# A hybrid pooling/SSD decoder step on one core: earlier operand loads, one operand's low halves on another engine, and paired weight chunks in the second FFN product

## The chip, the core and the metric

The kernel runs on one core of one Trainium2 chip. A core has a matrix engine (TensorE, PE in the profile, with its weight loads shown as PEld), a vector engine (VectorE, DVE), a scalar engine (ScalarE, ACT), a general engine (GpSimd, POOL) and a queue engine (SyncE, SP) from which this kernel issues nearly all its transfers. The metric is device microseconds for one execution, the median of several runs.

## The reference: what is computed

One layer of a decoder trunk for a prompt of 1024 tokens and 64 sample tokens (8 sequences of 8), width 1024: a half-step SwiGLU FFN, a token mixer of two branches (causal pooling and a Mamba-2 SSD scan) merged by gates, a second half-step SwiGLU FFN, and a final RMSNorm.

```
def swiglu(x, w_in, w_out):
    gu = x @ w_in
    g, u = gu[..., :D_FF], gu[..., D_FF:]
    return (jax.nn.silu(g) * u) @ w_out          # D_FF = 2816, D_MODEL = 1024

x = x + 0.5 * swiglu(rmsnorm(x, norm_ffn1), ffn1_w_in, ffn1_w_out)
x = x + token_mixing(rmsnorm(x, norm_mix), ...)
x = x + 0.5 * swiglu(rmsnorm(x, norm_ffn2), ffn2_w_in, ffn2_w_out)
```

All arrays are float32. The change lies in the product with `w_out` alone, which runs twice, once in each FFN.

## The kernel before, in words

Every matrix product is done in three passes of a reduced-precision float32 type (F32R): an operand is split into a high half, a rounded copy made by ScalarE, and a low half, the difference, made as a rule by VectorE. The passes are high times high, weights' high times operand's low, and weights' low times operand's high.

The product with `w_out` is done "by sevens" (Strassen's scheme): both operands are cut in two by two blocks, and seven products of sums of blocks replace eight. `second` (from L767) runs the seven in the order `ORDER2 = "4251736"`; below they are called the first to the seventh product. The sums on the operand's side were formed earlier and lie in DRAM as `xq[p][kk]`, 11 tiles of 128x544 for each product (272 KB each). The sums on the weights' side are formed as they are needed. A product has two passes (`m0` = 0 and 2, each for 256 output columns), and a pass goes through 22 halves of the inner size in six **chunks**: five of two K-tiles and one of a single K-tile. For a chunk `second_weights` (L747 to L765) loads one or two raw blocks by SP (tile `wraw`, 256 KB a block, 6 buffers); where there are two, POOL adds or subtracts them into `ws` (L759, tag `wsum`, 4 buffers); ACT makes the high half `wh` (L763) and DVE the low half `wl` (L764), 3 buffers each. The first product ("4") and the sixth ("3") use a single raw block and have no sum on POOL; the other five use two.

With a chunk's weights there, PE (L177) runs, for each of two output tiles `j` and each K-tile, six matmuls of 272 columns: twelve for one `j` of a two-tile chunk, 24 a chunk, 264 a product. The results of a pass lie in four PSUM banks (two `j`, two column halves `c`); after a pass `add` (L810) scales them and adds them to the FFN's output tiles, mostly on DVE (L825, "evictions" below). In the sixth and seventh product all four banks come from a ring of six, so that the second `j` of a pass reuses the two banks of the first `j` of the pass before.

The operand of the next product is fetched while one runs (`fetch_x`, L772). Each step issues one load on SP (L786); the split into `hh`/`hp` (high, ACT, L776) and low half in place (L777) is emitted `X_LAG` = 4 steps later. The first step is due `X_AT` = 4.0 us (of modelled PE time) into the running product, and the steps are `X_PACE` = 1.8 us apart; for the last operand the delay is 15.0 and the pace 1.4. Operand tiles lie in a ring of 42 buffers (`act`), or, for products "4", "5" and "7", mostly in 8 pair buffers; a load waits until the earlier content has been read by PE. For the seventh product alone (`LO_POOL = "6"`) the low halves are made by POOL.

What is emitted in this order is then arranged by the framework's scheduler, which sets a fixed order for each engine's queue from its own estimates. At run time every engine takes its queue strictly in that order: an instruction that waits holds all behind it. On SP that means that an operand load that waits for its buffer holds the weight loads behind it, and on ACT that a split that waits for its load holds the next `wh`.

## Time and profile before

| what | value |
|---|---|
| median of 3 runs | 2902.27 us (2901.49 to 2903.34) |
| the profiled execution | 2906.4 us |
| its span, first to last instruction | 2904.6 us |
| PE busy in the span | 2788.6 us (96%) |
| second product of the first FFN | 528.7 to 787.7 us, 1848 matmuls |
| second product of the second FFN | 2624.1 to 2889.0 us, 1848 matmuls |

The profile shows one execution. Busy time of PE is that of pipelined matmuls, so the idle time in front of a matmul says more than the busy share: the view of waits gives, for each engine, how long it sat idle before an instruction and which other engine's instruction ended that wait. Since each stage has other limits, the views are read stage by stage, by windows in microseconds from the start of the span. In the first FFN the seven products begin at 528.7, 565.2, 599.4, 636.5, 672.1, 709.1 and 744.4 us; in the second at 2624.1, 2661.7, 2697.4, 2733.8, 2768.9, 2811.4 and 2850.9 us.

### The profile page before, as it was taken

To read this page: it belongs to the slowest core of one execution; us is meant where nothing else is said; L and a number is where in the kernel's file an instruction comes from. 1 tells how busy PE (TensorE), PEld (TensorE's weight loads), DVE (VectorE), ACT (ScalarE), POOL (GpSimd) and SP (SyncE) were. 2 spreads that over 40 slices of the span, in tenths; PEclk is the share of its full clock that TensorE was granted. 3 is DMA by queue.
4 is the path that set the end of the run, shared out by engine and by line. 5 is a ranking of instruction groups with operands and counts; after the bars stand their busy time and mean duration, and the time that the engine had idled before them with its cause. 6 is when DMAs were issued, how large, how long until landed. Compare 5 with 4: busy or idle time off the path is not lost. (4 is left out here: it accounts for less than half of the span.)

```text
span 2904.6 us, 54721 instructions
## 1 busy us (share of the span) xinstructions
PE 2788.6 (96%) x19834; PEld 2607.3 (90%) x19834; DVE 1878.8 (65%) x2890; ACT 1413.8 (49%) x3150; POOL 1400.8 (48%) x1428
## 2 busy tenths in 40 slices
PE   7999999999999999999999999899999999999997
PEld 6999999899889999999988887578999999999997
DVE  6556555776874586876766777766665454556754
ACT  5444444543454565554556566576233434445433
POOL 6566667442642355564622343332135666673424
PEclk9999999999999999999999999999999999999999
DMA  4565554787745455543376677785765332337855
GB/s 136 181 206 193 170 169 146 253 284 230 242 128 159 155 173 160 187 155 125 106 250 203 202 230 234 254 265 175 250 233 162 102 105 90 97 120 260 295 168 177
DMA packets 515791, 539.49 MB, mean 186 GB/s; under 512 B 41780, under 2 KB 356008, under 8 KB 515512
## 3 DMA queue, kind: packets, MB, share of 16 engines
q1 hardware_dynamic: 515504, 535.99, 57.6%
q8 instruction: 156, 2.56, 0.4%
q14 instruction: 115, 0.94, 0.1%
q10 hardware_dynamic: 16, 0.00, 0.0%
HBM read 383.43 MB, written 152.65 MB: 185 GB/s over the span
## 5 line engine op out<-in xcount | busy, mean ns | idle before, releaser
L177 PE MATMUL pw<-X,wh 128*128 128x288 f32 (+2 forms) x2832 | 627.4, 310 | 5.0 <-ACT v L576 2.6
L177 PEld LDWEIGHTS pw<-X,wh 128*128 128x128 f32 x2832 | 462.5, 190 | 26.9 <-ACT v L576 3.3
L177 PE MATMUL pw<-X,wl 128*128 128x288 f32 (+1 forms) x1644 | 473.8, 288 | 0.7 <-DVE wl L459 0.7
L459 DVE TENSOR_TENSOR wl<-s,wh 128x512 fp32r<-128x512 f32 x288 | 242.9, 845 | 248.3 <-ACT wh L458 237.0
L177 PE MATMUL pw<-hl,wh 128*128 128x256 f32 (+1 forms) x1536 | 391.6, 328 | 3.5 <-ACT t L580 2.3
L452 POOL TENSOR_TENSOR s<-wraw,wraw 128x512 f32<-128x512 f32 x144 | 198.1, 1376 | 331.6 <-DVE wl L459 215.0
L177 PE MATMUL pw<-hi,wh 128*128 128x288 f32 x1120 | 331.7, 296 | 2.7 <-DVE t L616 2.0
L177 PE MATMUL pw<-hi,wl 128*128 128x288 f32 x1120 | 329.8, 294 | 0.0
L177 PE MATMUL pw<-lo,wh 128*128 128x288 f32 x1120 | 329.7, 294 | 0.0
L177 PEld LDWEIGHTS pw<-X,wl 128*128 128x128 f32 x1644 | 311.8, 190 | 0.9 <-DVE wl L459 0.9
L177 PE MATMUL pw<-hl,wl 128*128 128x256 f32 x1072 | 300.6, 280 | 1.2 <-DVE wl L459 1.2
L177 PEld LDWEIGHTS pw<-hl,wh 128*128 128x128 f32 x1536 | 258.8, 189 | 24.7 <-ACT t L580 2.9
L759 POOL TENSOR_TENSOR ws<-wraw,wraw 128x512 f32<-128x512 f32 x120 | 166.9, 1399 | 225.1 <-DMA wraw<-in_ffn_w_out_dram 126.5
L459 DVE TENSOR_TENSOR wl<-wraw,wh 128x512 fp32r<-128x512 f32 x216 | 178.6, 827 | 123.3 <-ACT wh L458 121.0
L458 ACT ACTIVATE wh<-s 128x512 fp32r<-128x512 f32 x288 | 181.0, 629 | 137.9 <-PE pw L177 111.7
L177 PEld LDWEIGHTS pw<-hi,wh 128*128 128x128 f32 x1120 | 210.5, 188 | 9.6 <-DVE t L616 2.6
L177 PEld LDWEIGHTS pw<-lo,wh 128*128 128x128 f32 x1120 | 210.6, 188 | 0.0
L458 ACT ACTIVATE wh<-wraw 128x512 fp32r<-128x512 f32 x216 | 135.6, 628 | 154.0 <-PE pw L177 133.6
L177 PEld LDWEIGHTS pw<-hi,wl 128*128 128x128 f32 x1120 | 210.1, 188 | 0.0
L177 PEld LDWEIGHTS pw<-hl,wl 128*128 128x128 f32 x1072 | 203.0, 189 | 2.1 <-DVE wl L459 2.1
L177 PE MATMUL po<-hh,wh 128*128 128x272 f32 x848 | 180.2, 293 | 10.6 <-ACT wh L763 6.5
L177 PE MATMUL po<-hh,wl 128*128 128x272 f32 x848 | 178.9, 292 | 8.3 <-DVE wl L764 7.7
(403 smaller groups left out, 6872.9 us busy)
## 6 DMA issues: line engine op xcount, KB each, us to landing
wraw<-in_ffn_w_out_dram SPq DMA_DIRECT2D x240, 256.0 KB
wraw<-in_ffn_w_in_dram SPq DMA_DIRECT2D x188, 256.0 KB
wraw<-in_w_in_dram SPq DMA_DIRECT2D x144, 256.0 KB
wh<-part SPq DMA_DIRECT2D x116, 256.0 KB
wl<-part SPq DMA_DIRECT2D x116, 256.0 KB
hr<-xq SPq DMA_DIRECT2D x106, 272.0 KB
xq<-s SPq DMA_DIRECT2D x66, 272.0 KB
xq<-g SPq DMA_DIRECT2D x62, 272.0 KB
```

Source lines behind the costliest of these rows:

```text
L177: T.matmul(out, lhsT, rhs, start=start, stop=stop, skip_group_check=free)
L452: G.tensor_tensor(t, a, b, op=op)
L458: S.activation(wh, a, AF.Copy)
L459: V.tensor_tensor(wl, a, wh.bitcast(F32), op=ALU.subtract)
L759: G.tensor_tensor(s, raws[0], raws[1], op=ALU.subtract if p in MINUS2 else ALU.add)
```

## The change

Four things change in the second product, in both FFNs.

1. Operand loads: the first step comes 2.0 us into a product instead of 4.0, steps are 1.6 apart instead of 1.8, and the split is emitted six steps after the load instead of four. The last operand keeps a lag of four, its delay and its pace.
2. The low halves of the seventh product's operand are made by DVE instead of POOL: 11 instructions in each FFN.
3. The weights of single-block products (the first and the sixth) take their `wh` and `wl` from the `wsum` ring for two chunks in five, and from the rings of three for the other three.
4. In the sixth and seventh product the first two and the last two chunks of a pass are run as a pair: both chunks' weights are made, and then PE does all K-tiles of both for the first `j` and then for the second. A pass starts with 24 matmuls and ends with 18 on one `j`, instead of 12 and 6.

```diff
-LO_POOL = "6"
-X_AT, X_PACE, X_LAG = 4.0, 1.8, 4
+X_AT, X_PACE, X_LAG, X_LAG_END = 2.0, 1.6, 6, 4
...
             else:
                 s = raws[0]
-            wh, wl = (sp.tile([P, 4 * P], F32R, tag=t, bufs=N_W, name=nm(t))[:, : n2 * 2 * P] for t in ("wh", "wl"))
+            nth[0] += len(raws) == 1
+            if len(raws) > 1 or nth[0] % 5 < 3:
+                wh, wl = (sp.tile([P, 4 * P], F32R, tag=t, bufs=N_W, name=nm(t))[:, : n2 * 2 * P] for t in ("wh", "wl"))
+            else:
+                wh, wl = (stage["p"].tile([P, 4 * P], F32R, tag="wsum", bufs=N_S, name=nm(t))[:, : n2 * 2 * P] for t in ("wh", "wl"))
...
-                (G if p in LO_POOL else V).tensor_tensor(t[:, :n].bitcast(F32R), t[:, :n], a[:, :n].bitcast(F32), op=ALU.subtract)
+                V.tensor_tensor(t[:, :n].bitcast(F32R), t[:, :n], a[:, :n].bitcast(F32), op=ALU.subtract)
...
-                ahead.append(start(fetch_x(ORDER2[at + 1], range(NKK), 1.4 if last else X_PACE), 15.0 if last else X_AT if at else 6.0))
+                ahead.append(start(fetch_x(ORDER2[at + 1], range(NKK), *((1.4, X_LAG_END) if last else (X_PACE, X_LAG))),
+                                   15.0 if last else X_AT if at else 6.0))
...
-                for kp in range(0, NKK, 2):
-                    n2 = min(2, NKK - kp)
-                    W2 = second_weights(wo, p, kp, n2, m0)
+                kps = [(kp,) for kp in range(0, NKK, 2)]
+                if at >= 5:
+                    kps = [kps[0] + kps[1]] + kps[2:-2] + [kps[-2] + kps[-1]]
+                for run in kps:
+                    W2 = [(kp, min(2, NKK - kp), second_weights(wo, p, kp, min(2, NKK - kp), m0)) for kp in run]
                     for j in range(2):
-                        for k in range(n2):
+                        for kp, n2, W in W2:
+                            for k in range(n2):
...
```

The rest of the loop's body is the same with other indices. The change moves instructions on the queues; three places follow. Line numbers shift: L759, L763, L764, L776, L786 and L825 of the kernel before are L758, L766, L767, L779, L789 and L828 of the changed one.

The first place is ACT in the second FFN about the start of the fifth product (2764 to 2778 us). `hh_34198`, `hh_34231` and `hh_34265` are the splits of K-tiles 8, 9 and 10 of the sixth product's operand; `wh_33925` is the fifth product's second chunk and `wh_33964` its third. Before:

```order
L763 ACTIVATE wh_33887<-ws_33885 128x512
...
L776 ACTIVATE hh_34173<-hr_34172 128x544
L776 ACTIVATE hh_34198<-hr_34197 128x544
L763 ACTIVATE wh_33925<-ws_33923 128x512
L776 ACTIVATE hh_34231<-hr_34230 128x544
L763 ACTIVATE wh_33964<-ws_33962 128x512
L776 ACTIVATE hh_34265<-hr_34264 128x544
L763 ACTIVATE wh_34006<-ws_34004 128x512
```

Their loads on SP, before (`wraw_34116` and `wraw_34118` are the seventh chunk's blocks):

```order
L753 DMA wraw_34116<-in_ffn_w_out_dram 128x2x256
L753 DMA wraw_34118<-in_ffn_w_out_dram 128x2x256
L786 DMA hr_34197<-xq_8_337 128x544
L786 DMA hr_34230<-xq_9_338 128x544
L786 DMA hr_34264<-xq_10_339 128x544
```

The same two places after the change, ACT first (`wh_33926` and `wh_33967` are the second and third chunk) and then SP (`wraw_34003` to `wraw_34043` are the fourth and fifth chunk's blocks, `wraw_34080` and `wraw_34082` the sixth's, `wraw_34117` and `wraw_34119` the seventh's):

```order
L766 ACTIVATE wh_33885<-ws_33883 128x512
...
L779 ACTIVATE hh_34174<-hr_34173 128x544
L766 ACTIVATE wh_33926<-ws_33924 128x512
L779 ACTIVATE hh_34197<-hr_34196 128x544
L766 ACTIVATE wh_33967<-ws_33965 128x512
L766 ACTIVATE wh_34009<-ws_34007 128x512
```

```order
L789 DMA hr_34173<-xq_8_337 128x544
L752 DMA wraw_34003<-in_ffn_w_out_dram 128x2x256
...
L752 DMA wraw_34082<-in_ffn_w_out_dram 128x256
L789 DMA hr_34196<-xq_9_338 128x544
L803 DMA xr_34201<-xspill_3_94 128x576
L752 DMA wraw_34117<-in_ffn_w_out_dram 128x2x256
L752 DMA wraw_34119<-in_ffn_w_out_dram 128x2x256
L789 DMA hr_34231<-xq_10_339 128x544
```

K-tile 8 is now loaded four chunks earlier on SP and K-tile 9 one chunk earlier, K-tile 10 stays behind the seventh chunk's blocks, and its split has left the front of the fourth chunk's `wh`.

The second place is DVE in the first FFN from the sixth to the seventh product (about 744 us). `wl_9295` and `wl_9345` are the seventh product's first two weight chunks, the `x<-po` rows the evictions of the sixth product's second pass, `xn` and `hl` the norm in front of the mixer. Before:

```order
L764 TENSOR_TENSOR wl_9295<-ws_9292,wh_9294 128x512
L372 TENSOR_TENSOR hl_9323<-xn_9322,hl_9323 128x512
L965 SCALAR_TENSOR_TENSOR xn_9378<-x_6689,cols,r_9104 128x512
L764 TENSOR_TENSOR wl_9345<-ws_9342,wh_9344 128x512
L825 SCALAR_TENSOR_TENSOR x_6916<-po_9032,x_6916 128x272
L825 SCALAR_TENSOR_TENSOR x_6919<-po_9032,x_6919 128x272
```

After, where `hr<-hr,hh` are low halves that came from POOL and `wl_9305` is the second chunk:

```order
L780 TENSOR_TENSOR hr_9158<-hr_9158,hh_9159 128x544
L371 TENSOR_TENSOR hl_9260<-xn_9259,hl_9260 128x512
L828 SCALAR_TENSOR_TENSOR x_6912<-po_9032,x_6912 128x272
...
L828 SCALAR_TENSOR_TENSOR x_6925<-po_9035,x_6925 128x272
L767 TENSOR_TENSOR wl_9295<-ws_9292,wh_9294 128x512
L767 TENSOR_TENSOR wl_9305<-ws_9302,wh_9304 128x512
```

The eight evictions stood behind two `wl` and two norm steps, and now stand in front of the first `wl`.

The third place is POOL at the same point; in brackets stands whose progress the first sum of the seventh product waits for. Before, and then after:

```order
L759 TENSOR_TENSOR ws_9292<-wraw_9288,wraw_9290 128x512 [waits DMAHW7_49,DMAHW6_49,DVE_49]
```

```order
L758 TENSOR_TENSOR ws_9292<-wraw_9288,wraw_9290 128x512 [waits DMAHW6_49,DVE_49,DMAHW7_49,PE_49,Pool_49]
```

Since the sixth product's last two chunks now lie in the `wsum` ring, the first sums of the seventh take buffers that PE reads until nearly the end of the sixth; before, none of them waited for PE.

## The prediction

> **What bounds the kernel now.** I read the page's busy times, then the windows of the two second products, then PE's waits in each product, and last the timelines of the engine that each wait names.

> ```profile
> PE 2788.6 (96%) x19834; PEld 2607.3 (90%) x19834; DVE 1878.8 (65%) x2890; ACT 1413.8 (49%) x3150; POOL 1400.8 (48%) x1428
> ```
> ```profile
> core 0: us, PE busy (x) PEld busy (x) DVE busy (x) ACT busy (x) POOL busy (x), PEclk, DMA share, GB/s
> 528.00:565.00 37.00, 35.39 (x271) 34.26 (x269) 23.26 (x29) 17.43 (x39) 14.78 (x13) 1.00 0.80 262
> 565.00:599.00 34.00, 33.77 (x263) 33.18 (x262) 21.34 (x32) 17.70 (x41) 17.38 (x13) 1.00 0.94 311
> 744.00:788.00 44.00, 37.80 (x271) 36.23 (x269) 40.70 (x44) 19.51 (x36) 37.23 (x29) 0.92 0.80 252
> ```
> ```profile
> 2768.00:2811.00 43.00, 37.34 (x271) 36.80 (x270) 21.02 (x37) 9.20 (x16) 12.35 (x10) 0.88 0.47 151
> 2848.00:2889.00 41.00, 37.42 (x294) 36.56 (x293) 20.19 (x32) 13.07 (x27) 23.92 (x18) 1.00 0.42 128
> ```

> PE bounds the whole, so only its idle time can be saved. A product of 264 matmuls takes 34 us where it runs best (the first FFN's second product, at 94% DMA share), and 43 to 44 where it stalls. PE's waits in the products that the change aims at follow, in this order: first FFN, first, fifth and seventh product (windows 528 to 565, 672 to 709, 744 to 790).

> ```profile
> PE po L177 <- DVE wl L764: 0.9, 1, 0.9
> PE po L177 <- ACT wh L763: 0.7, 1, 0.7
> ...
> PE po L177 <- ACT wh L763: 1.5, 1, 1.5
> PE po L177 <- DVE wl L764: 1.0, 1, 1.0
> ...
> PE po L177 <- DVE x L825: 3.5, 1, 3.5
> PE po L177 <- DVE wl L764: 2.6, 2, 2.1
> ```

> Second FFN, first, fifth and seventh product (2624 to 2662, 2768 to 2811, 2848 to 2890):

> ```profile
> PE po L177 <- ACT wh L763: 2.4, 3, 1.6
> ...
> PE po L177 <- ACT wh L763: 4.1, 1, 4.1
> PE po L177 <- DVE wl L764: 1.6, 1, 1.6
> ...
> PE po L177 <- ACT wh L763: 2.0, 1, 2.0
> PE po L177 <- POOL hr L777: 1.4, 2, 0.7
> ```

> That is 1.6 and 2.4 us in the first products, 2.5 and 5.7 in the fifth, 6.1 and 3.4 in the seventh: 21.7 us in all, three quarters of a per cent of the span. In the fourth products, which have two such waits each, the change keeps the early place of the split that causes them:

> ```profile
> PE po L177 <- ACT wh L763: 1.0, 1, 1.0
> PE po L177 <- DVE wl L764: 0.9, 1, 0.9
> ```

> **Operand loads (part 1, and the spare weight buffers of part 3).** The 4.1 us in the second FFN's fifth product are seen whole in the timelines of ACT and SP:

> ```profile
> 2764.91 1.79 ACT L776 ACTIVATE hh<-hr 128x544 fp32r<-128x544 f32 x3
> 2774.99 0.66 ACT L776 ACTIVATE hh<-hr 128x544 fp32r<-128x544 f32 x1 [8.29 <-DMA hr<-xq]
> 2775.55 0.61 ACT L763 ACTIVATE wh<-ws 128x512 fp32r<-128x512 f32 x1
> ```
> ```profile
> 2761.94 3.15 SPq L753 DMA_DIRECT2D wraw<-in_ffn_w_out_dram  x4
> 2765.30 0.33 SPq L800 DMA_DIRECT2D xr<-xspill  x1
> 2769.49 0.89 SPq L753 DMA_DIRECT2D wraw<-in_ffn_w_out_dram  x2
> 2770.47 1.37 SPq L786 DMA_DIRECT2D hr<-xq  x3
> ```

> SP could issue K-tiles 8 to 10 only behind the seventh chunk's blocks, at 2770.47; the first was split at 2774.99, 4.5 us later. ACT stood at that split for 8.29 us with the second chunk's `wh` next in its queue, and behind it DVE's `wl` and PE. In the changed order K-tile 8 is issued ahead of the fourth chunk's blocks, before 2761.94, and K-tile 9 where the sixth chunk's end, at about 2765.3; with 4.5 us its split is possible at about 2770, and the third chunk's `wh` behind it is not needed before 2775, two chunks of 24 matmuls (6 us) after the product's start at 2768.9. K-tile 10 no longer stands in front. So this stall should go. The first FFN's fifth product has the same form (its K-tiles 8 to 10 behind the seventh and eighth chunks' blocks). I keep 1.0 of the two's 8.2 for what is late next, POOL's sums: gain **7.2** (0 if the wait only moves, 8.2 at most). In the first products, by the orders of SP and ACT, the second operand's splits now stand on average no chunk ahead of their loads instead of one and a half, and two chunks in five have a weight buffer more; of 1.6 + 2.4 = 4.0 I keep 1.0: gain **3.0** (0 to 4.0). The second to fourth products (1.9 in each fourth, little elsewhere) I leave, at gain 0.

> What it costs: nothing is added to SP's queue, but loads in each product stand ahead of weight blocks that were ahead of them. For crowding I take **1.0** lost in all; the bounds are in the rivals.

> **Low halves by DVE, and pairs (parts 2 and 4).** First the prices:

> ```profile
> L777 POOL TENSOR_TENSOR hr<-hr,hh 128x544 fp32r<-128x544 f32 x11 | 18.1, 1663 | 6.3 <-ACT hh L776 6.1
> ```
> ```profile
> 745.26 1.83 DVE L764 TENSOR_TENSOR wl<-ws,wh 128x512 fp32r<-128x512 f32 x1
> ...
> 748.77 1.81 DVE L965 SCALAR_TENSOR_TENSOR xn<-x,cols,r 128x512 f32<-128x512 f32 x1
> 750.51 0.68 DVE L764 TENSOR_TENSOR wl<-ws,wh 128x512 fp32r<-128x512 f32 x1
> 751.11 2.86 DVE L825 SCALAR_TENSOR_TENSOR x<-po,x 128x272 f32<-128x272 f32 x8
> ```
> ```profile
> 744.72 5.32 POOL L777 TENSOR_TENSOR hr<-hr,hh 128x544 fp32r<-128x544 f32 x3 [0.59 <-ACT hh L776]
> ```

> The same DVE subtraction takes 0.68 us when POOL rests and 1.83 when it falls on one of POOL's (744.72 to 750.04). So 11 low halves leave POOL (18.1 us in the first FFN) and add 11 x 0.7 = 7.7 us to DVE at least, 11 x 1.83 = 20 at most; each DVE step that no longer falls on one of POOL's gets 1.15 back, 11 x 1.15 = 12.7 at most. I take the two as even: DVE is about as busy as before at this place, and POOL free. [...]

> In the first FFN the seventh product's start lost 2.1 us at `wl` (745.26, slow, and behind norm steps) and 3.5 at the evictions of the sixth, which DVE reached only at 751.11. Both go: the evictions now stand before the `wl`, and with pairs a pass gives 18 matmuls' time at its end and 24 at its start to free the banks, instead of 6 and 12. A matmul takes 0.125 us, from the chain of waits:

> ```profile
> 2815.75 1.50 PE po L177 x12
> ```

> so the room grows from 18 to 42 matmuls, 2.25 to 5.25 us, against 2.86 for eight evictions. In the second FFN:

> ```profile
> 2842.13 6.81 POOL L777 TENSOR_TENSOR hr<-hr,hh 128x544 fp32r<-128x544 f32 x5 [1.48 <-ACT hh L776]
> 2848.90 4.19 POOL L759 TENSOR_TENSOR ws<-wraw,wraw 128x512 f32<-128x512 f32 x3
> ```

> POOL came to the seventh product's first sums only after six low halves: the 2.0 us. The 1.4 us are PE waiting for POOL's later low halves. Both causes go.

> A new wait comes in their place. The first sum now waits for the `wsum` buffer of the sixth product's eleventh chunk. PE reads its `wh` last 8 matmuls before the end, 1.0 us; then the sum (4.19 / 3 = 1.4) and `wh` (0.61): PE's first matmul is 1.0 late. Four matmuls on (0.5), it needs `wl`, which takes 0.68 to 1.83, so 0.2 to 1.3 more. POOL's second sum and all behind it are queued on that wait, but are needed only 12 matmuls later. I take **2.2** each, near the slow row, since POOL's second sum runs just then. Gain 6.1 + 3.4 - 2 x 2.2 = **5.1** (7.1 at the fast rows; 0 if each start costs 4.75).

> **Given back.** PE's gain up to the end of the first FFN is about 6 us, and DVE, at 40.70 of 44.00 us in its last product, is to have the mixer's first operands ready that much sooner. I take **1.5** lost there (0 to 6). The second FFN's gain is passed on to the end whole, since the last output follows its last matmul.

> Sum: 7.2 + 3.0 + 5.1 - 1.0 - 1.5 = 12.8 us. Against the profiled execution that is a span of 2904.6 - 12.8 = 2891.8 and a time of 2906.4 - 12.8 = 2893.6. This execution was 4.1 us over the median of the runs, 2902.27; against the median the sum gives 2889.5, and I say **2890**.

> **Rivals.** *Only the last product pays.* Operand loads wait for buffers that PE frees, so naming them earlier need not make them land earlier; ACT then waits at another split. For it: the fourth products' early splits are where they were. Against: K-tile 8 moves past four chunks on SP. Gain 5.1 - 1.5 = 3.6: 2898.7.

> *Crowding makes it slower.* In the second, third and fourth products the 16 DMA engines are nearly full: 0.94 at 311 GB/s in the second. An operand tile of 272 KB takes 0.9 us at that rate; with the first step 2.0 us sooner and steps closer, one or two more stand ahead of a weight block, up to 1.8 us, and POOL's sums, `wh`, `wl` and PE are queued behind. If that comes through once in each of six products it costs 10.8. From 13.8 / 6 = 2.3 each it beats all gains above, or from 3.6 / 6 = 0.6 each where the loads gain nothing; then the time is 2902.3 + 10.8 - 3.6 = 2909.5. Against: those products run at 34 to 36 us, with weights up to three chunks ahead. [...]

> *All stalls before the seventh product go*, those of the fourths (3.8) too: 4.0 + 8.2 + 3.8 + 5.1 - 1.5 = 19.6, 2882.7.

> **Chances.** Forecast 0.55 (2884 to 2896), only the last product 0.20, crowding 0.10, all stalls 0.15. A change under 0.2% (5.8 us, 2896.5 to 2908.1) can hardly be told from none here. Faster: 0.15 and nearly all of 0.55, 0.67. Same: 0.20, a little of the forecast and a little of crowding, 0.24. Slower: 0.09. The range, 2881 to 2902, leaves out crowding and the ends.

> **What would show it.** Right: no wait of ACT near 8 us at the fifth product, no eviction row and no `hr` row among PE's waits in the seventh, 11 low halves on DVE near 0.7 to 1.8 us, POOL's first sum of the seventh waiting for PE and a stall of 1 to 2.5 us there, and products two to four at 34 to 36 us. Wrong: those at 37 or more (crowding), a stall over 3 us in a fifth product, one over 4 at the seventh's start, or new waits of PE at the mixer's beginning over 3 us.

## The result, and the profile after

The changed kernel takes 2880.72 us in the median of six runs (2873.33 to 2881.9), the kernel before on the same chip 2900.14 (2897.9 to 2903.34): a ratio of 0.9929, 95% interval 0.9918 to 0.9939, about 20 us faster. The forecast of 2890 had the sign; the gain came out at 20 instead of 12.8 us, just under the range's lower end. The profiled execution of the changed kernel took 2876.8 us with a span of 2875.0. It lies 4 us under its median, as that of before lay above, so differences between these two traces (29.6 us) are larger than the gain.

The page's busy times, and the windows of the changed kernel's fourth, fifth, sixth and seventh product (first FFN, then second; the columns are those of the prediction's windows):

```profile
PE 2777.4 (97%) x19834; PEld 2600.5 (90%) x19834; DVE 1887.1 (66%) x2912; ACT 1411.0 (49%) x3150; POOL 1377.5 (48%) x1406
```
```profile
core 0: us, PE busy (x) PEld busy (x) DVE busy (x) ACT busy (x) POOL busy (x), PEclk, DMA share, GB/s
...
635.30:669.20 33.90, 33.82 (x265) 33.60 (x266) 32.58 (x49) 16.78 (x32) 17.45 (x12) 1.00 0.94 300
669.20:703.40 34.20, 33.67 (x267) 33.46 (x266) 22.81 (x40) 10.51 (x19) 11.09 (x10) 1.00 0.70 218
703.40:739.70 36.30, 34.72 (x279) 34.50 (x277) 26.25 (x54) 15.41 (x27) 3.99 (x3) 1.00 0.71 231
739.70:779.40 39.70, 36.21 (x265) 35.32 (x266) 37.45 (x42) 16.62 (x31) 28.41 (x24) 0.96 0.82 257
...
2717.90:2751.80 33.90, 33.82 (x265) 33.61 (x266) 32.33 (x49) 16.77 (x32) 17.11 (x12) 1.00 0.93 301
2751.80:2786.00 34.20, 33.67 (x267) 33.45 (x266) 22.26 (x38) 8.93 (x16) 11.96 (x10) 1.00 0.58 187
2786.00:2823.90 37.90, 37.09 (x302) 36.86 (x300) 25.23 (x54) 16.86 (x36) 3.40 (x3) 1.00 0.63 212
2823.90:2859.40 35.50, 35.50 (x283) 35.50 (x284) 22.14 (x30) 12.07 (x26) 15.36 (x11) 1.00 0.42 128
```

The fourth and fifth products now take 33.9 and 34.2 us in both FFNs, at a clock of 1.00. The second FFN's fifth took 42.4 before (first matmul to the next product's), at a clock of 0.88. Only the first FFN's seventh still stands out, with 39.7 us, a clock of 0.96, and DVE busy for 37.45 of them.

PE's waits after, in the first FFN's fifth product and from the end of its sixth to the end of its seventh (669.2 to 703.4, 738 to 779.6), then in the same two places of the second FFN (2751.8 to 2786, 2822 to 2860):

```profile
PE po L176 <- DVE wl L767: 0.5, 1, 0.5
```
```profile
PE po L176 <- DVE hr L780: 2.3, 1, 2.3
PE po L176 <- ACT wh L766: 1.6, 1, 1.6
PE po L176 <- DVE wl L767: 1.1, 1, 1.1
```
```profile
PE po L176 <- DVE wl L767: 0.5, 1, 0.5
```
```profile
PE po L176 <- ACT wh L766: 0.8, 1, 0.8
```

The 8.2 us of the two fifth products have become 1.0. In the seventh products the evictions and POOL's low halves are gone from the list, and the wait that the prediction announced (POOL's first sum, now behind PE) is there with 1.6 and 0.8 us. New is a wait of 2.3 us for DVE's own low half of the operand, in the first FFN.

A second profile was taken of each kernel (spans 2898.4 and 2874.7). The table gives the seven products, from first matmul to the next product's first (the seventh to its own last), as the mean of the two profiles of each kernel, and the gain over both FFNs:

| product | 1 | 2 | 3 | 4 | 5 | 6 | 7 |
|---|---|---|---|---|---|---|---|
| first FFN, before | 36.8 | 34.7 | 36.9 | 35.9 | 36.1 | 35.0 | 42.7 |
| first FFN, after | 35.2 | 34.8 | 36.8 | 33.9 | 34.2 | 36.3 | 39.6 |
| second FFN, before | 37.2 | 35.7 | 36.4 | 35.3 | 42.6 | 39.5 | 37.7 |
| second FFN, after | 35.6 | 35.8 | 35.9 | 33.9 | 33.8 | 37.9 | 35.3 |
| gain, both | 3.2 | -0.2 | 0.6 | 3.4 | 10.7 | 0.3 | 5.5 |

That sums to 23.5 us. What lies between the two second products took 1836.6 and 1834.2 us before, 1832.2 and 1832.9 after.

### The profile page after: what moved, and what is told of

Its sections match the earlier page's. It is cut to its first block, busy times and chain, and to the rows that moved or that the text cites. A ratio compares the mean times of both kernels' runs of the same rounds, so it can differ in the third digit from the quotient of the medians.

```text
span 2875.0 us, 54724 instructions
## 1 busy us (share of the span) xinstructions
PE 2777.4 (97%) x19834; PEld 2600.5 (90%) x19834; DVE 1887.1 (66%) x2912; ACT 1411.0 (49%) x3150; POOL 1377.5 (48%) x1406
## 5 line engine op out<-in xcount | busy, mean ns | idle before, releaser
L758 POOL TENSOR_TENSOR ws<-wraw,wraw 128x512 f32<-128x512 f32 x120 | 177.5, 1486 | 200.5 <-DMA wraw<-in_ffn_w_out_dram 88.7
L176 PE MATMUL pso<-yhl,wh 128*128 128x288 f32 (+1 forms) x768 | 178.0, 337 | 5.0 <-ACT acc L1752 4.4
```

Of the source, the lines that this page charges most:

```text
L176: T.matmul(out, lhsT, rhs, start=start, stop=stop, skip_group_check=free)
L758: G.tensor_tensor(s, raws[0], raws[1], op=ALU.subtract if p in MINUS2 else ALU.add)
```

## The experiments

All kernels compute the whole function. The times are ratios to the kernel before, run on the same chip in the same session, with their 95% intervals; the gain in us is (1 - ratio) x 2900. The parts are numbered as in the change: 1 the operand loads, 2 the low halves by DVE, 3 the spare weight buffers, 4 the pairs.

| parts kept | ratio | interval | gain, us |
|---|---|---|---|
| all four, first session | 0.9929 | 0.9918 to 0.9939 | 20.6 |
| all four, a later session | 0.9935 | 0.9922 to 0.9947 | 18.9 |
| 2, 3, 4 (no loads) | 0.9988 | 0.9979 to 0.9997 | 3.5 |
| 1, 3 (no low halves, no pairs) | 0.9977 | 0.9969 to 0.9986 | 6.7 |
| 1, 2, 4 (no spare buffers) | 0.9948 | 0.9931 to 0.9964 | 15.1 |
| 1 alone | 0.9956 | 0.9944 to 0.9968 | 12.8 |
| 1, 3, 4 (no low halves) | 0.9981 | 0.9972 to 0.9989 | 5.5 |
| 1, 2, 3 (no pairs) | 0.9936 | 0.9924 to 0.9948 | 18.6 |
| 1, 2 | 0.9930 | 0.9916 to 0.9944 | 20.3 |

**Is the stall in the second FFN's fifth product the kernel's own?** Before, unchanged, and the change without part 1:

> The kernel before, unchanged, for a second profile of it. If its stall in the second FFN's fifth product (4.1 us idle, clock 0.88) belongs to the kernel, it is there again, 3 to 5 us, with a clock under 0.95; if it was one late transfer, that product is 35 to 38 us long.

```diff
-X_AT, X_PACE, X_LAG, X_LAG_END = 2.0, 1.6, 6, 4
+X_AT, X_PACE, X_LAG, X_LAG_END = 4.0, 1.8, 4, 4
```

> The changed kernel with the operand loads as before (first step 4.0 us into a product, steps 1.8 apart, split four steps after the load); the other three parts stay. First theory (the prediction's sum, idle time only): the stalls of the first and fifth products come back, 10.2 us, so about 2891, and the fourth products do not change. Second theory (a long stall also lowers the granted clock of PE behind it): the second FFN's fifth product is 42 us long again, 5 to 6 us of it idle and 2 to 3 more at a clock under 0.95; with the fourth products' stalls of 3 us back as well, 2893 to 2897. Third theory (the profile of the kernel before caught an unusually late transfer): no stall over 2 us in a fifth product, 2881 to 2885.

The product was 42.7 us long in the second profile of before (42.4 in the first), with a wait of 3.8 us for `wh`. Without part 1 it is 42.9 us long, and the kernel is at 0.9988. The wait is there again (2761.7 to 2804.7):

```profile
PE po L176 <- ACT wh L766: 3.9, 1, 3.9
```

So it is no single late transfer, and the loads are what takes it away: the second theory. The clock in it, in five pieces of the first trace of before:

```profile
2770.66:2774.08 3.42, 1.47 (x12) 1.25 (x10) 0.00 (x0) 0.00 (x0) 0.05 (x1) 1.00 0.90 275
2774.08:2777.49 3.41, 1.27 (x5) 1.27 (x6) 1.81 (x6) 2.50 (x5) 0.00 (x0) 0.50 1.01 346
2777.49:2780.90 3.41, 1.83 (x9) 1.51 (x8) 3.41 (x10) 0.81 (x2) 0.90 (x1) 0.50 0.43 166
2780.90:2784.32 3.42, 3.42 (x17) 3.42 (x17) 3.42 (x3) 0.63 (x1) 3.42 (x3) 0.50 0.50 160
2784.32:2787.73 3.41, 3.41 (x29) 3.41 (x29) 3.41 (x5) 0.42 (x1) 1.48 (x2) 1.00 0.87 277
```

In the first piece PE is idle for 1.95 us; three pieces at 0.50 follow. In the last of these PE does 17 matmuls in the time of 29, though nothing keeps it waiting.

**The loads alone.** The kernel before with part 1 only:

> The kernel before with the earlier operand loads alone (first step 2.0, pace 1.6, split six steps after the load, last operand four); low halves of the seventh product on POOL, all weights in the rings of three, no pairs. If the parts add up by stage as the profiles of before and after differ (fourth products 3.1, fifth 11.0): 0.9945 to 0.9955 of the kernel before, 13 to 16 us faster, with no stall over 1 us in a fourth or fifth product. If the loads need the other parts (without pairs and DVE's low halves a stall of 6 us stood before the first FFN's seventh product, without spare weight buffers one of 5.9 us before its second): both stalls are there, 12 us of the gain are given back, and it is 0.998 to 1.000.

0.9956: 12.8 us (9.3 to 16.2), just under the 13 to 16 expected. In its trace the fourth products (634.4 to 668.2, 2719.7 to 2753.6) have one wait, 1.0 us at their start, the fifth (668.2 to 701.7, 2753.6 to 2787) run without a stop, and its first FFN's seventh product (737 to 780.1) stalls as before:

```profile
634.40:668.20 33.80, 33.73 (x264) 33.50 (x265) 30.07 (x49) 16.41 (x31) 17.85 (x13) 1.00 0.91 303
668.20:701.70 33.50, 33.50 (x267) 33.50 (x266) 21.91 (x38) 10.06 (x18) 10.53 (x8) 1.00 0.66 213
737.00:780.10 43.10, 36.62 (x267) 35.61 (x266) 38.66 (x44) 18.93 (x35) 35.98 (x28) 0.92 0.78 250
...
2753.60:2787.00 33.40, 33.40 (x266) 33.40 (x265) 21.12 (x36) 8.29 (x15) 10.27 (x9) 1.00 0.57 183
```
```profile
PE po L176 <- DVE x L828: 3.5, 1, 3.5
PE po L176 <- DVE wl L767: 2.8, 2, 2.2
```

The stalls that the second expectation feared, 6 us at each of two places, are not there as such: a wait of 3.4 us stands at the end of the second FFN's first product, one of 1.0 at that of the first FFN's.

**Low halves and pairs.** Both undone, and each by itself:

```diff
-                V.tensor_tensor(t[:, :n].bitcast(F32R), ...
+                (G if p == "6" else V).tensor_tensor(t[:, :n].bitcast(F32R), ...
...
-                if at >= 5:
+                if at >= 9:
```

> The changed kernel with the seventh product's low halves back on POOL and without the pairs of chunks; loads and spare weight buffers stay. The prediction's sum: 5.1 us back, about 2886. With the clock: the first FFN's seventh product is 43 us long at a clock near 0.92, 6 to 7 us back, 2887 to 2888. If the last product owed its gain to the earlier loads alone: within 2 us of the changed kernel, 2881 to 2883.

> The changed kernel with the seventh product's low halves on POOL again, pairs kept. If POOL's low halves, standing ahead of its first sums, cause the 6 us in front of the first FFN's seventh product: that stall stays, about 5 to 8 us slower than the changed kernel. If the pairs alone cure it: within 2 us of the changed kernel, with POOL's low halves among PE's waits.

> The changed kernel without the pairs of chunks, low halves on DVE. If the pairs give the evictions the room that the prediction worked out: PE waits again for evictions of the sixth product in the first FFN's seventh, 2 to 4 us idle and 1.7 to 3.4 us of clock behind it, 3 to 6 us slower than the changed kernel. If DVE reaches the evictions in time since they now stand ahead of the weights' low halves: no such wait, within 2 us.

Without part 2, pairs or not, 12 to 15 us of the gain are lost, far more than the 5.1 of the prediction and more than any of these expectations; without part 4 no loss can be seen. The longest wait stands at the start of the first FFN's seventh product, here first without both and then without part 2:

```profile
PE po L176 <- ACT wh L766: 6.1, 1, 6.1
```
```profile
PE po L176 <- ACT wh L766: 9.1, 1, 9.1
```

Beside the changed kernel's profiles the first FFN's sixth and seventh product together are 6 and 10 us longer, and the second FFN's 4 and 2. POOL's timeline before that place, first with the loads alone, then with parts 1, 3 and 4:

```profile
720.98 1.91 POOL L758 TENSOR_TENSOR ws<-wraw,wraw 128x512 f32<-128x512 f32 x1 [34.60 <-DVE x L828]
...
726.87 1.30 POOL L758 TENSOR_TENSOR ws<-wraw,wraw 128x512 f32<-128x512 f32 x1 [2.55 <-DMA wraw<-in_ffn_w_out_dram]
728.12 3.57 POOL L780 TENSOR_TENSOR hr<-hr,hh 128x544 fp32r<-128x544 f32 x2
```
```profile
726.99 6.73 POOL L780 TENSOR_TENSOR hr<-hr,hh 128x544 fp32r<-128x544 f32 x4 [5.04 <-ACT hh L779]
735.56 1.34 POOL L780 TENSOR_TENSOR hr<-hr,hh 128x544 fp32r<-128x544 f32 x1 [1.84 <-ACT hh L779]
738.74 4.38 POOL L780 TENSOR_TENSOR hr<-hr,hh 128x544 fp32r<-128x544 f32 x3 [1.83 <-ACT hh L779]
743.08 2.94 POOL L758 TENSOR_TENSOR ws<-wraw,wraw 128x512 f32<-128x512 f32 x2
```

Without spare buffers POOL makes the seventh product's first two sums at 720.98 and 726.87, ahead of its low halves. With them the sums must wait for PE, and the fixed order puts them behind eight low halves, which themselves wait for their splits (5.04, 1.84 and 1.83 us in the rows). So the dear thing is part 3 without part 2: the spare buffers put a wait into POOL's queue, and POOL's low halves turn it into 9 us. That is one reason why the losses from undoing single parts add up to more than the whole gain.

The pairs were to give the evictions room. Without them (parts 1, 2, 3) the first FFN's seventh product has no eviction among its waits either (735 to 778):

```profile
PE po L176 <- ACT wh L766: 2.0, 2, 1.6
PE po L176 <- DVE wl L767: 1.1, 1, 1.1
```

**The low halves without the other two parts.** Parts 1 and 2 only:

> The changed kernel without the spare weight buffers and without the pairs: earlier loads, and all low halves on DVE. If the low halves only pay together with the spare buffers (whose wait in POOL's queue is what POOL's low halves make dear): the same as the loads alone, 0.9945 to 0.9965 of the kernel before, with a long stall at the end of the first product as without the spare buffers. If they pay alone what the prediction gave to them: 0.993 to 0.994.

0.9930 (0.9916 to 0.9944), as much as the whole change: the low halves pay by themselves, and no stall over 2 us stands at the end of the first products. (The second FFN's second product has a wait of 2.5 us for `wl` in this trace and is 38.9 us long.) PE's waits in its first FFN's seventh product (735 to 776):

```profile
PE po L176 <- DVE hr L780: 2.9, 3, 1.7
PE po L176 <- DVE x L828: 0.9, 1, 0.9
```

Against the loads alone the eviction wait has fallen from 3.5 to 0.9 us without any pairs.

**Without the spare buffers, all else kept.**

```diff
-            if len(raws) > 1 or nth[0] % 5 < 3:
+            if True:
```

> The changed kernel with all single-block weights in the rings of three, as before. If the wait that the spare buffers bring costs what the trace shows (POOL's first sum of the seventh product waiting for PE, stalls of 1.6 and 0.8 us): those two stalls go, 2.4 us less, unless the first products need the buffers. If the spare buffers carry the gain of the first products (3 us): 2881 to 2884. Between: 2878 to 2884.

0.9948 (0.9931 to 0.9964); it could be as good as the whole change or 10 us worse, and its six times (2874.98 to 2887.36) spread wide. In the profiled one the two stalls at the seventh products' starts became 0 and 1.6 us, so the second grew, and in the first FFN's seventh product PE waited 4.5 us for `hr` instead of 2.3; the longest wait, 5.9 us, came at the end of the first FFN's first product. POOL's sum for the next product took 7.18 us there, while DVE worked without a pause:

```profile
556.11 7.18 POOL L758 TENSOR_TENSOR ws<-wraw,wraw 128x512 f32<-128x512 f32 x1 [16.21 <-DMA wraw<-in_ffn_w_out_dram]
```
```profile
554.76 3.27 DVE L780 TENSOR_TENSOR hr<-hr,hh 128x544 fp32r<-128x544 f32 x5
557.94 0.69 DVE L767 TENSOR_TENSOR wl<-wraw,wh 128x512 fp32r<-128x512 f32 x1
558.54 2.00 DVE L780 TENSOR_TENSOR hr<-hr,hh 128x544 fp32r<-128x544 f32 x3
560.45 0.42 DVE L767 TENSOR_TENSOR wl<-wraw,wh 128x256 fp32r<-128x256 f32 x1
560.78 1.36 DVE L780 TENSOR_TENSOR hp<-hp 128x544 fp32r<-128x544 f32 x2
```

Parts 1 and 2 alone have no spare buffers either; there the same sum took 1.48 us and no such stall came:

```profile
553.62 1.48 POOL L758 TENSOR_TENSOR ws<-wraw,wraw 128x512 f32<-128x512 f32 x1 [16.25 <-DMA wraw<-in_ffn_w_out_dram]
```

So the 5.9 us do not show that spare buffers are needed. Nor are they shown to be useless: with earlier loads and no spare buffers two of the six first products in three traces end in such a stall (this one, and 3.4 us with the loads alone) and are 40.1 and 37.9 us long, the other four 34.4 to 35.7; with both, the 22 in eleven traces are 34.7 to 36.9 long.

**Better versions.** Four were tried. The first keeps the last four chunks of the sixth product out of the spare ring; the second adds POOL for three low halves in the first FFN, the third instead puts the last operand's splits ahead of the norm steps, the fourth is the first without pairs:

```diff
-            if len(raws) > 1 or nth[0] % 5 < 3:
+            if len(raws) > 1 or nth[0] % 5 < 3 or p == "3" and m0 == 2 and kp >= 4:
...
-                V.tensor_tensor(t[:, :n].bitcast(F32R), ...
+                (G if half is None and p == "6" and kk in (5, 7, 9) else V).tensor_tensor(t[:, :n].bitcast(F32R), ...
...
+                with tc.high_priority(HP_EV if p == "6" else 0):
                     S.activation(a[:, :n], t[:, :n], AF.Identity)
```

> The changed kernel once more, for a second profile and for a time beside the two variants that share its chip. 0.992 to 0.994 of the kernel before on any chip; by stage the same as in its first profile: fifth products 34 us, first FFN's seventh 39 to 40 us with a stall of 2 us or more and one stretch of 3.4 us at half clock.

> The changed kernel, but the last four chunks of the sixth product's second pass take their weights from the rings of three, so that POOL's first sums of the seventh product wait for no matmul. If that wait costs what the changed kernel's trace shows: its two stalls (1.6 and 0.8 us) go and the time falls by 1.5 to 2.5 us. Rival: the sixth product's own weights then come late, or the seventh product is bound by DVE in the first FFN anyway: within 1 us of the changed kernel.

> As the kernel with the last four chunks in the rings of three, and in the first FFN three of the eleven low halves of the last operand (K-tiles 5, 7 and 9) are made by POOL again. If DVE's share of the work delays the low half at 757.8 us (2.3 us of stall and 3.4 us at half clock behind it): that stall goes, 2 to 4 us less than without this. If what POOL does slows DVE as much as it relieves it: no gain, or 1 to 3 us more.

> As the kernel with the last four chunks of the sixth product in the rings of three, and the splits of the last operand go ahead of the norm steps on ACT and DVE (higher priority). If the order on DVE is what delays the low half in the first FFN's seventh product: no stall on a low half there, and no half clock, 2 to 4 us less than the variant without the priority. If DVE is simply full there: the norm ends later instead, the mixer starts later by as much, and nothing is gained.

> The changed kernel without the pairs, and with the last four chunks of the sixth product in the rings of three. If the pairs pay nothing and the wait of POOL's first sum costs 1.5 to 2.5 us: 0.992 to 0.993 of the kernel before, 1 to 3 us less than the changed kernel. Rival: without the pairs and without the wait the evictions of the sixth product stand behind the new weights on DVE again, PE waits 2 us or more for them in the first FFN's seventh product, and it is 0.994 or more.

The changed kernel's second profile is as expected: fifth products of 34.1 and 33.4 us, 40 in the first FFN's seventh, with a stall of 3.3 for `hr` and one stretch at half clock. The four reached 0.9924 (0.9909 to 0.9938), 0.9925 (0.9912 to 0.9937), 0.9931 (0.9919 to 0.9943) and 0.9936 (0.9924 to 0.9949), against 0.9935 (0.9922 to 0.9947) for the changed kernel in the session of the first two. No interval is clear of the changed kernel's. In the first one the two waits for POOL's first sum went as intended, and PE then waited in the same product for DVE instead (734 to 776):

```profile
PE po L176 <- DVE hr L780: 3.0, 3, 2.0
PE po L176 <- DVE wl L767: 1.0, 1, 1.0
```

DVE is nearly full in the first FFN's seventh product (busy for 37.45 of 39.70 us in the changed kernel), and of the 1.6 us taken from POOL 0.7 came back at DVE (3.0 for `hr` instead of 2.3). In the second the waits there were spread over `wl` (2.4 us), POOL's low halves (1.8) and DVE's (1.6), and did not go. The priority of the third moved nothing there (3.1 us for `hr`). In the fourth the rival's wait showed itself, 2.2 us for an eviction in that product, but not its time of 0.994 or more: that pairs save time where POOL's wait is gone is not shown.

**What a stall costs.** In the changed kernel, run once each time, PE was held up on purpose between the two passes of the second, fourth and fifth products, by a tiny matmul (whose result is overwritten) that waits for a chain of small ACT copies:

```diff
+                if m0 and at in DOSE[half is None]:
+                    with tc.high_priority(HP_EV):
+                        for q in range(DOSE[half is None][at]):
+                            S.copy(z[q % 2], z[1 - q % 2] if q else before[1][1][:, :8])
+                    mm(pts[0][0][:8, :8], z[1 - DOSE[half is None][at] % 2], z[1 - DOSE[half is None][at] % 2])
+                before = pts
```

> The changed kernel with PE held up once on purpose, between the two passes, in the second, fourth and fifth product of each FFN: a tiny matmul waits for a chain of small ACT copies that begins when the first pass's first bank is done (6, 8 and 10 copies in the first FFN, 12, 14 and 18 in the second; stalls of some 1.4 to 4.4 us). If a stall costs its length alone: the granted clock stays at 1.00 behind all of them. If a stall past some length also costs clock: behind the longer ones 3.4 us or a multiple at 0.50, which adds 1.7 us each, and behind the shorter ones nothing; the traces so far put the border between 1.4 and 2.1 us.

> The changed kernel with PE held up on purpose between the two passes of the second, fourth and fifth products, as in the first attempt, but the chain of ACT copies (0.21 us each; 5, 8 and 11 in the first FFN, 14, 18 and 22 in the second) begins only when the last bank of the first pass is done, so the stalls should be 1.5, 2, 2.7, 3.3, 4.2 and 5 us. If a stall costs its length alone, these products are longer than in the changed kernel by the stall and no more, at a clock of 1.00. If half clock follows from PE's idle time within one 3.41 us stretch of a fixed grid: the stalls from 2.7 us up are each followed by one to three stretches at 0.50 and cost 1.5 to 3.5 us over their length; that of 1.5 us costs its length; that of 2 us either.

The first attempt started its chains at the first bank (`before[0][0]`), too early: five of six stalls were 1.1 us or less, the sixth 2.1, and no half clock followed. The second gave 1.0, 0 and 0.4 us in the first FFN, 0.9, 2.7 and 2.1 in the second, again shorter than meant. The two long ones were each followed by one stretch at 0.50, as the second case expected; stalls over 2.7 us were not reached. The pieces of the second attempt's trace around the 2.7 and the 2.1, and of the first attempt's around its 2.1:

```profile
2744.74:2748.15 3.41, 0.71 (x7) 0.46 (x6) 2.63 (x3) 2.56 (x13) 0.78 (x1) 1.00 1.07 362
2748.15:2751.56 3.41, 3.41 (x17) 3.41 (x16) 1.31 (x2) 1.29 (x2) 0.00 (x0) 0.50 1.08 365
...
2782.29:2785.70 3.41, 1.27 (x11) 1.02 (x11) 0.00 (x0) 2.45 (x13) 0.00 (x0) 1.00 0.00 0
2785.70:2789.11 3.41, 3.41 (x17) 3.41 (x17) 0.69 (x1) 0.63 (x1) 0.00 (x0) 0.50 0.02 5
2789.11:2792.52 3.41, 3.41 (x29) 3.41 (x29) 1.60 (x3) 1.57 (x3) 0.00 (x0) 1.00 0.26 78
```
```profile
2742.19:2745.60 3.41, 2.85 (x23) 2.63 (x21) 3.41 (x12) 2.20 (x12) 0.75 (x1) 1.00 1.03 330
2745.60:2749.02 3.42, 1.91 (x16) 1.88 (x17) 3.42 (x5) 2.24 (x7) 1.75 (x1) 1.00 1.05 359
2749.02:2752.43 3.41, 3.41 (x30) 3.41 (x29) 3.39 (x4) 1.66 (x3) 1.73 (x1) 1.00 1.06 380
```

The second FFN's fourth and fifth products have no half clock in the two profiles of the changed kernel (1.00 in the windows of the first, above), so the stall causes it. The 2.1 us that cost no clock fell across a border (0.56 us idle in one piece, 1.51 in the next), and that product, the second FFN's fourth, became 36.3 us long instead of 33.9. The 2.1 us inside one piece cost 12 of 29 matmuls (0.125 us each, from the prediction's row of twelve in 1.50 us), 1.5 us, on top of themselves: the second FFN's fifth product became 37.4 us long instead of 33.8. The product with the 2.7 us has other new waits too (1.7 us for `wl`), so its length gives no price.

## Why the prediction was right and where it was wrong

**Operand loads, gain 7.2 in the fifth products: idle time right, price of a stall wrong.** The idle time fell from 8.2 to 1.0 (mean of two profiles of each kernel: 7.3 to 0.7). The ACT wait of 8.29 us is gone as worked out (the longest there for a load is now 2.6), and the rival "only the last product pays" fell with it. But the products became 10.7 us shorter. The step that failed is "PE bounds the whole, so only its idle time can be saved", and with it the 21.7 us: it counted a stall at its idle time. The rows with clocks of 0.88 and 0.92 stood among the prediction's own windows and were not used. Of the gain, 10.7 less the 6.6 of idle time, 4 us, is matmuls that ran slow behind a stall, most of it half clock (10.2 us at 0.50 in the second FFN's).

**The fourth products, "at gain 0": wrong.** They gained 3.4 us. Of their two waits the one at the start stayed (1.1 and 1.2 us after; the table counts it to the third product), as argued. The other, 0.9 us for `wl`, went in both, though the prediction held that the change keeps the early split that causes such waits. It came, like the fifth's, from splits that stood behind their loads: before, ACT waited 2.70 and 1.71 us for loads of the fifth product's operand at 640.5 and 644.5, with the next `wh` behind, and that operand too is now fetched earlier. That the loads do it is shown: alone they bring these products to 33.9, and without them they are 36.9 and 35.3. The two waits make 1.8 of the 3.4; the rest is, in the first profile of before, the matmuls next to them (from one matmul to the next 1.21 us and then 0.23, where 0.125 is usual, so that a wait of 0.9 costs 1.2) and, in the first FFN, four steps of 0.23 to 0.42 us at 645.9, whose 0.6 us the view of waits leaves out. Applying the fifth's argument to all products, as the rival "all stalls before the seventh product go" did, was right here: its 2882.7 is the nearest of the four. That it is so near is in part luck, since it too counts a stall at its idle time.

**First products, gain 3.0:** 3.2 measured. What the prediction gave to loads and spare buffers together, each can do alone: the kernel without the loads has 34.9 and 35.3 us there (36.8 and 37.2 before), parts 1 and 2 without spare buffers 35.2 and 34.8.

**Crowding, -1.0:** no loss. The second and third products gained 0.4 us in sum, and the rival fell with that; the second products now run at up to 310 GB/s without a loss. The third are 36.5 and 36.8 us long in the first profile, between the prediction's sign for right (34 to 36) and that for wrong (37), as they were before (37.1 and 36.4). Nor were the 311 GB/s that the prediction called nearly full the most that was moved: four pieces of 3.41 us in the two attempts at stalls above moved 359 to 380.

**Low halves and pairs, 5.1:** 5.8 measured over the sixth and seventh products, near in sum, by luck, since the parts are wrong and their errors cancel. The first FFN was to give 6.1 - 2.2 = 3.9 and gave 1.8; the second was to give 1.2 and gave 4.0. The new wait of 2.2 each was mis-sized (1.6 and 0.8). "DVE is about as busy as before" held:

```profile
L780 DVE TENSOR_TENSOR hr<-hr,hh x11: 710/721/1816, 728.7 to 757.1; 128x544 fp32r<-128x544 f32 x11
```

Eleven low halves more, most at 0.72 us, and DVE is busy 37.45 of 39.70 us there, against 40.70 of 44.00 in the prediction's row. But being full it now delays a low half by 2.3 us, with half clock behind it (0.50 for 3.41 us from 758.87); this was not priced, and the prediction's sign of no `hr` row in the seventh product failed with it. And part 2 brings the gain without parts 3 and 4. That 18 matmuls at a pass's end and 24 at its start were needed to free the banks is not borne out: without pairs the waits for evictions went too, or fell to 0.9 us (2.2 in the fourth better version).

**Given back, -1.5:** not seen. The stretch between the two second products was no longer after than before (1832.2 and 1832.9 against 1836.6 and 1834.2); its spread from one execution to the next is as large as the term.

In sum the 12.8 lacked 3.5 in the fifth products, 3.4 in the fourth, 2.9 for the two deductions (the 1.5 did not come, and for crowding's 1.0 there was a gain of 0.4), and 0.9 in the first, sixth and seventh, to the 23.5 of the profiles. By the medians the gain is 18 to 21 only: the profiled executions of the kernel before took 4 to 6 us more than its medians, those of the changed kernel 4 to 5 less. So the table shows where the gain lies, and its sizes are somewhat large. The times of the experiments agree on the main step: the loads alone gave 12.8 us (9.3 to 16.2), where the prediction's terms for them, spare buffers included, come to 7.2 + 3.0 - 1.0 = 9.2.

What stays open: which of the waits at the borders of the first, second and third products are chance (they differ between two profiles of one kernel, and one of 4.2 us stands in the second FFN's third product without pairs), and whether spare buffers and pairs do anything that a finer measurement could tell.

## What to carry to other kernels

Price a stall of the matrix engine with what follows it: look at the granted clock in the windows behind the stall, not only at the wait. When an argument frees one stage (a load moved ahead of the weights on a shared queue), apply it to every stage of the same form before you leave one at zero. When several small changes go together, try each alone: here two of four were enough for the gain, and a third (the spare buffers) was harmful without the second (the low halves on DVE).

## What the runs showed of the hardware

**A sum on POOL took up to 7.18 us beside a run of DVE instructions.** In the prediction's rows a DVE subtraction took 1.83 us beside POOL's work and 0.68 without it. The reverse is larger. POOL's sum takes 1.28 to 1.30 us with less than 0.1 us of DVE work beside it (22 of them in the traces of before and after). In the trace without the spare buffers it took 7.18 us while DVE subtractions ran back to back (twelve from 554.76 to 562.14), and ended 1.15 us behind the last. In the changed kernel the same sum took 5.61, under eight that ended at 558.06, 1.16 us before it:

```profile
553.61 5.61 POOL L758 TENSOR_TENSOR ws<-wraw,wraw 128x512 f32<-128x512 f32 x1 [14.94 <-DVE hr L780]
```

With parts 1 and 2 alone it took 1.48. Of the 120 sums in the first trace of before none took over 1.85 us; of the 120 in that of after two took over 2, this one and one of 2.68 at 2835.71, under DVE work without a pause. Nine sums of 1.70 to 1.88 us in the two traces outlast the DVE work beside them, by 1.13 to 1.15 us. Why the instructions of the two engines lengthen beside each other was not tried.
